# Another order of VectorE's work in Strassen steps, and nine or ten of them in nine projections of a hybrid block

## The chip, the cores and the metric

The kernel runs on one core of one Trainium2 chip. Time is the device time of one execution in microseconds (us); the lower the better. A span is the time from the first to the last instruction of one profiled execution.

## The reference

One decoder block on 256 tokens with 4096 channels, float32. The input is normalized, projected by one large matrix, mixed in two branches, merged under sigmoid gates, projected again and normalized:

```python
h = rmsnorm(x, norm_w)
proj = h @ w_in                              # 4096 -> 6 * 2048 + 2 * 4096
u_p, z_p, u_c, b_c, c_c, z_c, g = split(proj)
y_pool = causal_multiscale_pool(u_p, pool_w, pool_scale) * silu(z_p)
y_conv = b_c * conv3(c_c * u_c) * silu(z_c)
br = [y_pool @ w_branch[0], y_conv @ w_branch[1]]
merged = sum(sigmoid(g + gate_b) * br)
out = rmsnorm(x + merged @ w_out, final_norm_w)
```

Nearly all of the work is in the three large products; the weights come from HBM once.

## The kernel before

**Units and steps.** The products are cut into units of 1024 output columns: cz, cb, cu, cc (twice) for the convolution branch, pz, pu (twice) for the pooling branch, g0_c and g1_c for the gates (c from 0 to 3), then b0_c and b1_c for the branch products and o0 to o3 for the output. A unit of the first product has 16 steps. A step takes 256 of the contracted channels (an "x pair", two blocks of 128 channels by two of 128 tokens) and one weight tile of 128 x 2048, which holds four quarters of 512 columns.

A float32 product is made of three matmuls of rounded operands: high x high, high x low, low x high, where low is the value less its rounded high. A plain step (P) has 8 block products, so 24 matmuls of 512 columns. A Strassen step (S) has 7 products of sums of blocks, so 21 matmuls; it needs four sums of the x blocks (Q3, Q5, Q6, Q7) beside the four blocks, and four sums of the weight quarters. The results of S collect in the `sums` banks (E) and the `shared` banks (F), which are put together at the unit's end ("corner sums", `corner_sums`, and `combine`).

**What prepares a step.** SyncE loads the weight tile into one of three `raw` tiles (L75). ScalarE rounds quarters to high parts in the `ring` tile (`highs`, L57), VectorE subtracts for the low parts (`lows`, L60). The ring has 15 cells, a cell being one quarter's high and low; P takes 4 cells, S takes 3 for quarters (`rounded`) and 4 for sums (`split`). Between these two, `added` makes the four sums of quarters in a tile `parts` (128 x 4 x 512). A cell is free again when TensorE has used it for the last time, so the ring bounds how far ScalarE and VectorE can run ahead. A raw tile is free when its last reader is done.

**Order.** Every engine works in program order. A planner at build time emits the instructions: `multiply` emits a step's matmuls, `pump` emits preparation for up to four steps ahead when ring cells are free, and `tick` (every 6 matmuls) emits one item of a queue of side work, such as a unit's epilogue (`epi`: activations, taps, transposes, stores) or a "fill", which loads a stored y or m block, makes its sums and its high and low parts. When a bank closes, `evacuate` has ScalarE copy it to SBUF; that copy stands in ScalarE's queue behind what was emitted before.

**Texts.** The order of P and S within a unit is a text of 16 letters (L36 to L46): FIRST and SIX4 for cz and pz0, EIGHT for cb, cc, pu, EIGHT3 for cu, HOST for pz1 and g0_0 (with steps of the pooling branch in between), NINE for the other gate units, SEVEN3 for g1_3. `seq_x` turns a text into x pairs: pairs 0 to 7 are laid out for P, pairs 8 to 15 for S. In a NINE unit pair 7 serves as the ninth S; its four sums stand in a tile of their own, `ninth` (128 x 2 x 4 x 128), which is made during g0_0 from a second load of the pair (`gate_unit`), and the class `Operand` finds them in `entry`. Pair 15 stands in a tile `last_pair`; all others in `arena`.

The places in the code that the change and the steps of the prediction touch: the texts (L36 to L46), `entry` (L186), `added` (L274) and `split` (L281), the table of products in `groups` (L305), `evacuate` (L386), `seq_x` (L488), `taps` (L527), `conv_units` (L513), `pool_units` (L550), `gate_unit` (L651), and the opening of tiles between units.

Of the kernel before, what the change touches and what calls it, by code (L numbers as in the profile page):

```python
# [9 lines left out]
F32 = mybir.dt.float32  # L10
# [27 lines left out]
SEVEN3 = "PPPSPSPSPSPSPSPS"  # L38
EIGHT3 = "PPPSSPSPSPSSPSPS"
EIGHT = "PSPSPSPSPSPSPSPS"  # L40
NINE = "PSPSPSPSSPSPSSPS"
HOST = "PPPBPPMMPSPSSPSSPSS"
OUT3 = "PSPSPSPSPSPSSPPP"
# [6 lines left out]
def hybrid_block(ctx: ExitStack, tc: tile.TileContext, x, xc, prm, rows_in, w_in, pool_w, w_branch, w_out, out):  # L50
# [89 lines left out]

    ninth = {}
    last_pair = {}
# [19 lines left out]
    class Operand:  # L162
# [23 lines left out]
        def entry(self, i):  # L186
            if self.kind == "P":
                return (ninth["tile"][:, 0, i], ninth["tile"][:, 1, i]) if i < 4 else (
                    self.view[:, 0, i - 4], self.view[:, 1, i - 4])
            return self.view[:, 0, i], self.view[:, 1, i]  # L190
# [44 lines left out]
    class Step:  # L235
# [25 lines left out]
        def rest(self):  # L261
# [11 lines left out]
            if self.kind == "S":  # L273
                def added(_):  # L274
                    q = self.q
                    add(sums[:, 0:2], q[:, 3:4].to_broadcast([P, 2, NH]), q[:, 1:3])
                    add(sums[:, 2], sums[:, 0], q[:, 2])
                    add(sums[:, 3], sums[:, 2], q[:, 0])
                    lows(self.cells, q[:, 0:3])

                def split(cells):  # L281
                    self.sum_cells = cells
                    highs(cells[0:2], sums[:, 0:2])
                    highs(cells[2:4], sums[:, 2:4])
                    lows(cells, sums)

                return [(None, None, added)] + self.mid + [(4, None, split)]
# [17 lines left out]
        def groups(self):  # L305
# [20 lines left out]
            else:  # L326
# [5 lines left out]
                         "N7": (Q7, w[0], ("F", 1, 0)),  # L332
                         "N6": (Q6, w[2], ("F", 1, 1)),
                         "N4": (A22, w[3], ("E", 1, 1))}
                order = ("M2", "N3", "N4", "M1", "N7", "N5", "N6") if self.closing else (
# [152 lines left out]
    def seq_x(text):  # L488
        if text is FIRST:
            return [("P", i) for i in FIRST]  # L490
        if text is NINE:
            ps, ss = list(range(ND - 1)), list(range(ND, ND + NS + NB)) + [ND - 1]
            return [(c, (ss if c == "S" else ps).pop(0)) for c in text]
        return sequence(text, ND, ND + NS + NB, NB)
# [18 lines left out]
    def conv_units(c, first):  # L513
# [7 lines left out]
        def c_epi(u):  # L521
# [21 lines left out]

        in_unit(f"cz{c}", base + 3 * HALF, lambda u: silu_y(False), FIRST if first else SIX4, dst=Y)
        in_unit(f"cb{c}", base + HALF, b_epi, EIGHT).urgent = lambda: mul(E, E, Y)
        u = in_unit(f"cu{c}", base, lambda u: rescale(Y) + (band_items(0) if c == 0 else []), EIGHT3, dst=Y)
        u.late, u.rotates = True, False
        in_unit(f"cc{c}", base + 2 * HALF, c_epi, EIGHT).urgent = lambda: mul(E, E, Y)

    def pool_units(c):  # L550
        u = in_unit(f"pz{c}", HALF + c * NU, lambda u: silu_y(c == 1) + (gap(4) + band_items(1) if c else []),
                    HOST if c else SIX4, dst=Y)
        if c:
            u.late, u.rotates = True, False
        in_unit(f"pu{c}", c * NU, lambda u: [], EIGHT).urgent = lambda: None

# [94 lines left out]
    def gate_unit(n, c):  # L651
        def epi(u):
            def bias(t):
                gather(E[:, t], gate_b[n, None, c * NU:(c + 1) * NU].to_broadcast([P, NU]))

            def ninth_in():
                move(sa[:, 4:].rearrange("p o c -> p (o c)"), xc[ND - 1])

            def ninth_scaled():
                for k in range(2):  # L660
                    v = sa[:, 6 - 2 * k:8 - 2 * k]
                    act(v, v, scale=norm_col(2 * (ND - 1) + k))

            def ninth_high():
                act(ninth["tile"][:, 0], sa[:, 0:4])

            def ninth_low():
                sub(ninth["tile"][:, 1], sa[:, 0:4], ninth["tile"][:, 0].bitcast(F32))

            pause = gap(12)  # L670
            if (n, c) == (0, 0):
                ninth_in()
                pause = [ninth_scaled, None, lambda: sums_s(sa)] + gap(3) + [ninth_high, None, ninth_low] + gap(3)
# [375 lines left out]
    def run_step(u, st):  # L1049
# [8 lines left out]
        for i, g in enumerate(gs):  # L1058
# [3 lines left out]
            after_group(u, g[0], st)  # L1062

    for u in units:
        if u.name == "b0_0":
# [4 lines left out]
        if u is names["g1_0"]:  # L1070
            bands_open.close()
            ninth["stack"] = ExitStack()
            ctx.enter_context(ninth["stack"])
            pool = ninth["stack"].enter_context(tc.tile_pool(name="ninth", bufs=1))
            ninth["tile"] = pool.tile([P, 2, 4, P], F32R, name="ninth")
        if u is last_x:
            ninth["stack"].close()
            more = ctx.enter_context(tc.tile_pool(name="more", bufs=1))
            stages.append(more.tile([P, 8, P], F32, name="sb"))
            queue_fills()  # L1080
        if u is last:
            break
        for st in u.steps:
# [24 lines left out]
    for st in lead:  # L1108
# [19 lines left out]
    def finish_half(t, n):  # L1128
# [3 lines left out]
            accum_out=ossq[:, t, 3 + n:4 + n])  # L1132
        mul(rest[:, t, cs], E[:, t, cs], Y[:, 0, cs])

    def finish(t):
        r = rout[:, t:t + 1]
        rstd_of(ossq[:, t:t + 1], r, f"rout{t}")
        for c in range(4):
            v = rest[:, t] if c == 3 else parked[c][:, t]
            if c == 1:  # L1140
# [3 lines left out]
        for c in (1, 0, 2, 3):  # L1144
            v = rest[:, t] if c == 3 else parked[c][:, t]
            queue_ = nc.scalar if c == 1 else nc.sync
# [53 lines left out]
```

## Time and profile before

| | |
|---|---|
| Median of three runs | 2384.67 us (2381.68 to 2386.14) |
| The profiled execution's own time | 2381.34 us |
| Its span | 2379.6 us |
| Granted TensorE clock, mean | 0.998 |
| HBM traffic over the span | 229 GB/s |

The profile names engines PE (TensorE's matmuls), PEld (its weight loads), DVE (VectorE), ACT (ScalarE), POOL (GpSimd) and SP (SyncE). A row of the timeline gives start in us, length in us, engine, line, operation, output<-input, shape and how many were merged into it; in brackets stands how long its engine was idle before it, and for whom. A group's row gives busy us and mean ns of one. L57, L60, L72 and L75 are the helpers that issue ScalarE's activations, VectorE's two kinds of elementwise operations and SyncE's loads; L999 is the matmul in `multiply`. Durations of matmuls overlap, so distances between starts are used for their pace. The lines themselves stand in the prediction.

### The profile page before, as it was taken

What the parts mean: (1) busy time and instruction counts of PE and PEld (TensorE: products, weight loads), DVE (VectorE), ACT (ScalarE), POOL (GpSimd) and SP (SyncE); (2) the same over time, 40 slices, a digit from 0 to 9 for tenths busy, and PEclk for the clock granted to TensorE, in tenths of its full rate; (3) what the DMA queues carried; (4) which work ended last, traced back from release to release, by engine and by line L of the source; (5) the groups of instructions that cost most, each with busy time, mean ns of one, the idle gap of its engine ahead of it and who ended that gap; (6) DMA issues with size and microseconds to landing.
All of it is one profiled execution on the core that took longest, in us unless ns stands there. A gap on an engine that the chain in (4) does not pass through costs nothing.

```text
span 2379.6 us, 26984 instructions
## 1 busy us (share of the span) xinstructions
PE 2362.8 (99%) x10493; PEld 1951.2 (82%) x10493; DVE 2147.0 (90%) x1793; ACT 1464.1 (62%) x1427; POOL 109.5 (5%) x168
## 2 busy tenths in 40 slices
PE   9999999999999999999999999999999999999998
PEld 7888888888888888888888888888878888888886
DVE  8789989989979969969999999998998798899998
ACT  6655656656656556656666666666665566566664
POOL 0000100000000000100000000001100000000000
PEclk9999999999999999999999999999999999999999
DMA  9646746656646646746877787678866666767767
GB/s 348 233 181 230 231 164 241 232 201 227 224 177 219 242 176 213 239 175 222 261 241 248 246 259 241 224 264 258 268 270 233 253 232 237 260 207 257 256 217 269
DMA packets 89056, 557.82 MB, mean 234 GB/s; under 512 B 9888, under 2 KB 10144, under 8 KB 28000
## 3 DMA queue, kind: packets, MB, share of 16 engines
q1 hardware_dynamic: 69824, 485.39, 56.3%
q0 software_dynamic: 18528, 69.48, 10.9%
q8 instruction: 82, 1.34, 0.2%
q10 hardware_dynamic: 576, 1.24, 0.1%
q14 instruction: 46, 0.38, 0.0%
HBM read 519.36 MB, written 26.21 MB: 229 GB/s over the span
## 4 chain that ended last, share of the span: by engine, by line
PE 89%; DVE 6%; ACT 2%; DMA 1%; issue 1%; SPq 0%; DVEq 0%; ACTq 0%
PE sums L999 66%; PE shared L999 21%; DVE ring L60 3%; DVE parts L60 1%; DMA raw<-in_w_in_dram 1%; PE shared L636 1%; ACT ring L57 1%; PE shared L444 1%; DVE Y L72 0%; DMA raw<-in_w_branch_dram 0%; ACT E L57 0%; DVE E L72 0%; ACT raw L57 0%; DVE raw L60 0%; DVE E L60 0%
## 5 line engine op out<-in xcount | busy, mean ns | idle before, releaser
L999 PE MATMUL sums<-ring,arena 128*128 128x512 f32 x7377 | 1721.0, 390 | 4.6 <-ACT E L57 3.0
L999 PEld LDWEIGHTS sums<-ring,arena 128*128 128x128 f32 x7377 | 1383.3, 188 | 294.5 <-ACT E L57 3.4
L60 DVE TENSOR_TENSOR ring<-raw,ring 128x1536 fp32r<-128x1536 f32 (+3 forms) x529 | 933.5, 1777 | 131.1 <-ACT ring L57 130.5
L57 ACT ACTIVATE ring<-raw 128x2048 fp32r<-128x2048 f32 (+3 forms) x528 | 786.6, 1506 | 407.8 <-PE sums L999 214.9
L57 ACT ACTIVATE ring<-parts 128x1024 fp32r<-128x1024 f32 (+1 forms) x427 | 421.3, 1002 | 366.3 <-DVE parts L60 328.9
L999 PE MATMUL shared<-ring,arena 128*128 128x512 f32 x2142 | 515.3, 389 | 0.0
L60 DVE TENSOR_TENSOR ring<-parts,ring 128x2048 fp32r<-128x2048 f32 (+3 forms) x243 | 458.5, 1901 | 30.4 <-ACT ring L57 29.9
L999 PEld LDWEIGHTS shared<-ring,arena 128*128 128x128 f32 x2142 | 402.0, 188 | 83.6
L60 DVE TENSOR_TENSOR parts<-parts,raw 128x512 f32<-128x512 f32 x398 | 275.8, 693 | 13.6
L60 DVE TENSOR_TENSOR parts<-raw 128x1024 f32<-128x1024 f32 x199 | 242.7, 1219 | 6.0 <-DMA raw<-in_w_in_dram 5.3
L999 PE MATMUL sums<-ring,last_pair 128*128 128x512 f32 x336 | 83.7, 396 | 0.0
L999 PEld LDWEIGHTS sums<-ring,last_pair 128*128 128x128 f32 x336 | 63.2, 188 | 15.1
L999 PE MATMUL shared<-ring,last_pair 128*128 128x512 f32 x192 | 47.6, 396 | 0.0
L57 ACT ACTIVATE E<-sums 128x512 f32<-128x512 f32 x72 | 41.8, 596 | 7.4 <-PE sums L999 3.5
L999 PEld LDWEIGHTS shared<-ring,last_pair 128*128 128x128 f32 x192 | 36.1, 188 | 8.8
L60 DVE TENSOR_TENSOR raw<-raw 128x512 f32<-128x512 f32 (+1 forms) x33 | 28.7, 869 | 9.1 <-ACT raw L57 8.3
L57 ACT ACTIVATE E<-sums,rin 128x512 f32<-128x512 f32 x28 | 17.8, 688 | 23.7 <-PE sums L999 23.7
L60 DVE TENSOR_TENSOR E<-E,Y 128x2048 f32<-128x2048 f32 x13 | 29.7, 2287 | 0.1
L84 POOL DMA_DIRECT2D E<-Y x14 | 17.0, 1452 | 260.6 <-DVE Y L60 125.0
L60 DVE TENSOR_TENSOR E<-E,last_pair 128x2048 f32<-128x2048 f32 x12 | 27.4, 2286 | 1.4 <-ACT E L57 1.4
L57 ACT ACTIVATE last_pair<-shared 128x512 f32<-128x512 f32 x44 | 24.0, 596 | 7.4 <-PE shared L444 6.5
L57 ACT ACTIVATE Y<-shared 128x512 f32<-128x512 f32 x44 | 23.9, 602 | 5.1 <-PE shared L444 4.6
(133 smaller groups left out, 674.4 us busy)
## 6 DMA issues: line engine op xcount, KB each, us to landing
raw<-in_w_in_dram SPq DMA_DIRECT2D x318, 1024.0 KB, 4.8
raw<-in_w_branch_dram SPq DMA_DIRECT2D x64, 1024.0 KB, 4.9
raw<-in_w_out_dram SPq DMA_DIRECT2D x64, 1024.0 KB, 5.0
E<-in_rows_dram POOLq DMA_DIRECT2D x16, 512.0 KB, 8.9
gates_d<-E POOLq DMA_DIRECT2D x8, 1024.0 KB, 6.8
E<-Y POOLq DMA_DIRECT2D x14, 512.0 KB, 10.0
y_d<-E POOLq DMA_DIRECT2D x8, 512.0 KB, 4.8
raw<-in_pool_w_dram SPq DMA_DIRECT2D x4, 1024.0 KB, 6.7
```

The source lines that it names most:

```text
L57: return pin(nc.scalar.activation(dst, src, func, **kw))
L60: return pin(nc.vector.tensor_tensor(out=dst, in0=a, in1=b, op=op))
L84: return pin(nc.gpsimd.dma_start(dst, src, accum_op=ALU.add))
L444: pin(nc.tensor.transpose(shared(j)[:, i * T + t * P:i * T + (t + 1) * P], src[:, t, c:c + P], ident))
L636: pin(nc.tensor.matmul(o, a, b, start=(k, i) == (0, 0), stop=(k, i) == (3, 2)))
L999: pin(nc.tensor.matmul(ps, lhs, rhs, start=n == 0, stop=n == u.total[b] - 1))
```

## The change

1. In an S step two of the four sums of weight quarters are no longer written to `parts` but over quarters 3 and 2 of the raw tile. VectorE's order becomes: the first two sums, the low of quarter 2, the third sum, the lows of quarters 0 and 1, the fourth sum, and after `split`'s three activations the lows of the sums in two halves. `parts` shrinks to two quarters (4 KB a partition less).
2. In the freed room a second tile `eighth` holds the four sums of x pair 7. It is made during cb0 (items behind cz0's epilogue). `ninth` now holds those of pair 6, made during g0_0 as before.
3. cb, cc and pu get nine S steps instead of eight (NINE_A, NINE_B), g0_1 to g0_3 ten instead of nine (TEN); g1_3 gets six instead of seven (SIX4). EIGHT3 (cu) keeps eight in another order.
4. The taps of cc's epilogue alternate between two blocks. The tail's `rest` tile becomes two tiles, with two loads and two adds.

```diff
-EIGHT3 = "PPPSSPSPSPSSPSPS"
+EIGHT3 = "PPPSPSPSSPSPSSPS"
 EIGHT = "PSPSPSPSPSPSPSPS"
 NINE = "PSPSPSPSSPSPSSPS"
+NINE_A = "PSPSSPSPSSPSPSPS"
+NINE_B = "PSPSPSPSSPSPSSPS"
+TEN = "PSPSSPSSPSSPSSPS"
...
-                return (ninth["tile"][:, 0, i], ninth["tile"][:, 1, i]) if i < 4 else (
-                    self.view[:, 0, i - 4], self.view[:, 1, i - 4])
+                sums_ = side[self.region[1]]
+                return (sums_[:, 0, i], sums_[:, 1, i]) if i < 4 else (self.view[:, 0, i - 4], self.view[:, 1, i - 4])
...
                 def added(_):
                     q = self.q
-                    add(sums[:, 0:2], q[:, 3:4].to_broadcast([P, 2, NH]), q[:, 1:3])
-                    add(sums[:, 2], sums[:, 0], q[:, 2])
-                    add(sums[:, 3], sums[:, 2], q[:, 0])
-                    lows(self.cells, q[:, 0:3])
+                    add(sums, q[:, 3:4].to_broadcast([P, 2, NH]), q[:, 1:3])
+                    lows(self.cells[2:3], q[:, 2:3])
+                    add(q[:, 3], sums[:, 0], q[:, 2])
+                    lows(self.cells[0:2], q[:, 0:2])
+                    add(q[:, 2], q[:, 3], q[:, 0])
 
                 def split(cells):
                     self.sum_cells = cells
-                    highs(cells[0:2], sums[:, 0:2])
-                    highs(cells[2:4], sums[:, 2:4])
-                    lows(cells, sums)
+                    highs(cells[0:2], sums)
+                    highs(cells[3:4], self.q[:, 3:4])
+                    highs(cells[2:3], self.q[:, 2:3])
+                    lows(cells[0:2], sums)
+                    lows(cells[2:4], self.q[:, 2:4])
...
-                         "N6": (Q6, w[2], ("F", 1, 1)),
-                         "N4": (A22, w[3], ("E", 1, 1))}
+                         "N6": (Q6, w[3], ("F", 1, 1)),
+                         "N4": (A22, w[2], ("E", 1, 1))}
...
-        if text is NINE:
-            ps, ss = list(range(ND - 1)), list(range(ND, ND + NS + NB)) + [ND - 1]
+        ns = text.count("S")
+        if ns > NS + NB:
+            ps, ss = list(range(16 - ns)), list(range(ND, 16)) + list(range(ND - 1, 15 - ns, -1))
...
+    def side_items(i):
+        def scaled():
+            for k in range(2):
+                v = sa[:, 6 - 2 * k:8 - 2 * k]
+                act(v, v, scale=norm_col(2 * i + k))
+
+        move(sa[:, 4:].rearrange("p o c -> p (o c)"), xc[i])
+        return [scaled, None, lambda: sums_s(sa)] + gap(3) + [
+            lambda: act(side[i][:, 0], sa[:, 0:4]), None,
+            lambda: sub(side[i][:, 1], sa[:, 0:4], side[i][:, 0].bitcast(F32))]
...
-                for i in range(2):
-                    b = 2 * j + i
-                    kb = 8 * c + b
-                    for s in (1, 2):
+                for s in (1, 2):
+                    for i in range(2):
+                        b = 2 * j + i
+                        kb = 8 * c + b
...
-        in_unit(f"cz{c}", base + 3 * HALF, lambda u: silu_y(False), FIRST if first else SIX4, dst=Y)
-        in_unit(f"cb{c}", base + HALF, b_epi, EIGHT).urgent = lambda: mul(E, E, Y)
+        in_unit(f"cz{c}", base + 3 * HALF, lambda u: silu_y(False) + (gap(4) + side_items(ND - 1) if first else []),
+                FIRST if first else SIX4, dst=Y)
+        in_unit(f"cb{c}", base + HALF, b_epi, NINE_B if c else NINE_A).urgent = lambda: mul(E, E, Y)
...
-        in_unit(f"cc{c}", base + 2 * HALF, c_epi, EIGHT).urgent = lambda: mul(E, E, Y)
+        in_unit(f"cc{c}", base + 2 * HALF, c_epi, NINE_A).urgent = lambda: mul(E, E, Y)
...
-        in_unit(f"pu{c}", c * NU, lambda u: [], EIGHT).urgent = lambda: None
+        in_unit(f"pu{c}", c * NU, lambda u: [], NINE_B).urgent = lambda: None
...
-        text = HOST if (n, c) == (0, 0) else SEVEN3 if (n, c) == (1, 3) else NINE
+        text = HOST if (n, c) == (0, 0) else SIX4 if (n, c) == (1, 3) else TEN if n == 0 else NINE
...
-                sums = ctx.enter_context(tc.tile_pool(name="parts", bufs=1)).tile([P, 4, NH], F32, name="parts")
+                _, sums = open_pool("parts", [P, 2, NH], F32)
+                eighth, side[ND - 1] = open_pool("eighth", [P, 2, 4, P], F32R)
...
-            rest = sums.rearrange("p (t a) n -> p t (a n)", t=2)
-            move(rest, xrows[:, :, 3 * NU:])
+            more.close()
+            eighth.close()
+            rest = [sums, open_pool("rest", [P, 2, NH], F32)[1]]
+            for t in range(2):
+                rest[t] = rest[t].rearrange("p a n -> p (a n)")
+                move(rest[t], xrows[:, t, 3 * NU:])
...
-            queue.extend([None] * 4 + [lambda: add(E, E, rest), lambda: act(root_, rin[:, 0:1], AF.Sqrt)])
+            queue.extend([None] * 4 + [lambda: [add(E[:, t], E[:, t], rest[t]) for t in range(2)], lambda: act(root_, rin[:, 0:1], AF.Sqrt)])
```

More of the change, by code (lines that the diff above doesn't have):

```diff
@@ L38 @@
 SEVEN3 = "PPPSPSPSPSPSPSPS"
-EIGHT3 = "PPPSSPSPSPSSPSPS"
+EIGHT3 = "PPPSPSPSSPSPSSPS"
 EIGHT = "PSPSPSPSPSPSPSPS"
 NINE = "PSPSPSPSSPSPSSPS"
+NINE_A = "PSPSSPSPSSPSPSPS"
+NINE_B = "PSPSPSPSSPSSPSPS"
+TEN = "PSPSSPSSPSSPSSPS"
 HOST = "PPPBPPMMPSPSSPSSPSS"
@@ L139, in hybrid_block @@
     LAST = ("s", NS + NB - 1)
-    ninth = {}
+    side = {}
     last_pair = {}
@@ L654, in bias @@
                 gather(E[:, t], gate_b[n, None, c * NU:(c + 1) * NU].to_broadcast([P, NU]))
[L656 to L673, printed above, removed]
+            pause = side_items(ND - 2) + gap(3) if (n, c) == (0, 0) else gap(12)
             return (rescale(E) if u.late else gap(1)) + [lambda: bias(0), lambda: bias(1)] + pause + [
@@ L1062, in run_step, with open_pool @@
             after_group(u, g[0], st)
+    def open_pool(name, shape, dt):
+        stack = ExitStack()
+        ctx.enter_context(stack)
+        return stack, stack.enter_context(tc.tile_pool(name=name, bufs=1)).tile(shape, dt, name=name)
     for u in units:
@@ L1071, in hybrid_block @@
             bands_open.close()
[L1072 to L1075, printed above, removed]
+            ninth, side[ND - 2] = open_pool("ninth", [P, 2, 4, P], F32R)
         if u is last_x:
-            ninth["stack"].close()
-            more = ctx.enter_context(tc.tile_pool(name="more", bufs=1))
-            stages.append(more.tile([P, 8, P], F32, name="sb"))
+            ninth.close()
+            more, second = open_pool("sb", [P, 8, P], F32)
+            stages.append(second)
             queue_fills()
@@ L1132, in finish_half @@
             accum_out=ossq[:, t, 3 + n:4 + n])
-        mul(rest[:, t, cs], E[:, t, cs], Y[:, 0, cs])
+        mul(rest[t][:, cs], E[:, t, cs], Y[:, 0, cs])
     def finish(t):
@@ L1138, in finish @@
         for c in range(4):
-            v = rest[:, t] if c == 3 else parked[c][:, t]
+            v = rest[t] if c == 3 else parked[c][:, t]
             if c == 1:
@@ L1144, in finish @@
         for c in (1, 0, 2, 3):
-            v = rest[:, t] if c == 3 else parked[c][:, t]
+            v = rest[t] if c == 3 else parked[c][:, t]
             queue_ = nc.scalar if c == 1 else nc.sync
```

## The prediction

> **What bounds the kernel now.** I read the page's head and chain first, then TensorE's waits, then the chain of work in order of time, then the windows of single projections.
>
> ```profile
> span 2379.6 us, 26984 instructions
> ...
> PE 2362.8 (99%) x10493; PEld 1951.2 (82%) x10493; DVE 2147.0 (90%) x1793; ACT 1464.1 (62%) x1427; POOL 109.5 (5%) x168
> ...
> PE 89%; DVE 6%; ACT 2%; DMA 1%; issue 1%; SPq 0%; DVEq 0%; ACTq 0%
> ```
> ```profile
> PE sums L999 <- ACT E L57: 3.0, 1, 3.0
> ...
> PE sums L999 <- ACT Y L57: 0.7, 2, 0.5
> ```
> ```profile
> 105.60 7.48 PE sums L999 x33
> ```
> The reader is to see a kernel that TensorE bounds: 99% busy, 89% of the chain, hardly a wait. Since matmuls overlap, their pace is read from the chain: 33 in 7.48 us, **0.2267 us each**. So a matmul less is worth 0.2267 us, as long as VectorE (90%) keeps its lead.
>
> ```profile
> 95.92:177.67 81.75, 81.75 (x361) 67.58 (x360) 65.85 (x48) 49.39 (x44) 0.00 (x0) 1.00 0.50 180
> 428.50:510.40 81.90, 81.88 (x360) 67.69 (x361) 72.73 (x54) 49.06 (x43) 0.00 (x0) 1.00 0.58 207
> 1204.72:1285.94 81.22, 81.22 (x358) 67.02 (x357) 76.36 (x59) 53.41 (x50) 4.71 (x5) 1.00 0.75 246
> 1611.00:1693.00 82.00, 82.00 (x362) 67.73 (x362) 74.54 (x67) 53.93 (x54) 10.87 (x16) 1.00 0.83 266
> 1693.30:1738.60 45.30, 42.34 (x187) 34.72 (x185) 41.03 (x45) 30.53 (x34) 5.58 (x9) 1.00 0.87 304
> ```
> These windows are cb0, cb1, g0_1, g1_3 and b0_0. Columns: length, then busy time of PE, PEld, DVE, ACT, POOL; GB/s last. VectorE is free for 15.9 us of cb0, 9.2 of cb1, 4.9 of g0_1.
>
> **TensorE's part.** A plain step is 24 matmuls, a Strassen step 21. Nine units get one more Strassen step (cb, cc and pu, two each, and g0_1 to g0_3), g1_3 one less: 8 x 3 = 24 matmuls, 24 x 0.2267 = **-5.44 us**.
>
> ```profile
> L999 PE MATMUL sums<-ring,arena 128*128 128x512 f32 x7377 | 1721.0, 390 | 4.6 <-ACT E L57 3.0 <-DVE ring L740 0.8 <-ACT Y L57 0.7
> ...
> L57 ACT ACTIVATE ring<-raw 128x2048 fp32r<-128x2048 f32 x204 | 390.9, 1917 | 175.3 <-PE sums L999 91.6 <-PE shared L999 25.1 <-DMA raw<-in_w_in_dram 20.4
> ...
> L57 ACT ACTIVATE ring<-raw 128x1536 fp32r<-128x1536 f32 x209 | 311.2, 1489 | 204.3 <-PE sums L999 113.4 <-DMA raw<-in_w_in_dram 44.3 <-issue 23.7
> ...
> L57 ACT ACTIVATE ring<-parts 128x512 fp32r<-128x512 f32 x58 | 33.6, 624 | 30.1 <-DVE parts L60 30.0
> ...
> L999 PE MATMUL shared<-ring,ninth 128*128 128x512 f32 x54 | 13.6, 396 | 0.0
> ```
> Matmuls whose weights lie in the separate tile of sums last 396 ns, not 390. Nine more steps use such a tile, 12 matmuls each: 108 x 6 ns = **+0.7 us** (0 to 1).
>
> **VectorE's part of a Strassen step.** The timeline gives the old order; a start-to-start distance is what an instruction really takes.
>
> ```profile
> 519.35 2.28 DVE L60 TENSOR_TENSOR ring<-raw,ring 128x2048 fp32r<-128x2048 f32 x1
> ...
> 521.55 1.22 DVE L60 TENSOR_TENSOR parts<-raw 128x1024 f32<-128x1024 f32 x1
> ...
> 522.80 1.42 DVE L60 TENSOR_TENSOR parts<-parts,raw 128x512 f32<-128x512 f32 x2
> ...
> 524.14 1.75 DVE L60 TENSOR_TENSOR ring<-raw,ring 128x1536 fp32r<-128x1536 f32 x1
> 524.32 1.07 ACT L57 ACTIVATE ring<-parts 128x1024 fp32r<-128x1024 f32 x1 [0.39 <-PE shared L444]
> ...
> 525.81 2.29 DVE L60 TENSOR_TENSOR ring<-parts,ring 128x2048 fp32r<-128x2048 f32 x1
> ...
> 528.13 1.23 DVE L60 TENSOR_TENSOR parts<-raw 128x1024 f32<-128x1024 f32 x1
> ```
> Old: 1.25 (add of 1024) + 1.34 (two adds) + 1.67 + 2.20 (2048, as at 519.35) = 6.46 us; a plain step is 2.20. Now what instructions cost that don't read their predecessor's result:
>
> ```profile
> 388.04 2.35 DVE L60 TENSOR_TENSOR ring<-raw,ring 128x1024 fp32r<-128x1024 f32 x2
> 390.31 1.91 DVE L72 SCALAR_TENSOR_TENSOR Y<-E,par,Y 128x255 f32<-128x255 f32 x4
> 392.13 1.22 DVE L60 TENSOR_TENSOR parts<-raw 128x1024 f32<-128x1024 f32 x1
> ```
> ```profile
> 532.40 2.29 DVE L60 TENSOR_TENSOR ring<-parts,ring 128x2048 fp32r<-128x2048 f32 x1
> ...
> 534.60 2.35 DVE L60 TENSOR_TENSOR ring<-raw,ring 128x512 fp32r<-128x512 f32 x2
> 534.78 2.43 PE L999 MATMUL shared<-ring,arena 128*128 128x512 f32 x10
> ```
> Two of 1024 end after 2.35, so the first took 2.35 - 1.22 = 1.13, against 1.25 for the add that the next one reads. The pair at 534.60 is 512 and 1536 wide: 2.35 - 1.75 = 0.60, while the first of two dependent adds took 1.42 - 0.69 = 0.73. The new order puts another instruction behind every add: 1.13 + 0.60 + 0.60 + 1.13 + 0.60 + 1.13 + 1.13 = 6.32. **VectorE gains 0.14 us per Strassen step**, although two instructions come in. The taps (1.82 us for four from 390.31) lose two such pairs, some 0.2 us a call. These gains lie beside TensorE and count only where VectorE is late.
>
> The Trainium skill, "VectorE: DVE Perf Modes", section "The DRAIN you can't avoid", speaks against this: the next operation waits until the pipe is empty, and authors are told to keep the number of operations small. The trace doesn't agree, by 1.25 against 1.13. By the page two more operations would cost two more fixed parts and win nothing, an estimate of some 6.6 us a step; this is rival C's mechanism.
>
> Does the lead hold? A ninth step adds 6.32 - 2.20 = 4.12 us; the others give back 8 x 0.14. cb1: 72.73 + 3.0 = 75.7 of 81.3 us. Ten in g0_1: 76.36 + 4.12 - 9 x 0.14 = 79.2 of 80.6. That is tight (1.4 us free), but the unit between two such units keeps nine steps and can win the lead back. So I put no stall there (bounds 0 and 2 us a unit; the upper one is five times the 0.4 us of ScalarE's queue, below). In cu the early pair of Strassen steps leaves little: the lows end at 532.40 + 2.29 = 534.69, and the matmuls from 534.78 on use them. The new text moves that pair back, which can only help.
>
> The second x pair's sums cost cb0 a DMA on POOL, three ScalarE instructions and, on VectorE, these two groups:
>
> ```profile
> 1711.08 1.02 DVE L60 TENSOR_TENSOR sa<-sa 128x128 f32<-128x128 f32 x4
> ```
> ```profile
> L60 DVE TENSOR_TENSOR ninth<-sa,ninth x1: 685/685/685, 1173.1 to 1173.1; 128x512 fp32r<-128x512 f32 x1
> ```
> That is 1.7 us, hidden in cb0's 15.9 free ones even beside its ninth step: nothing (1.7 us at most without that cover). POOL has 0.00 busy in cb0, so its DMA passes nothing; g0_0 prepares the other pair with the same instructions at the old place. The two-part tail (two adds for one of 2048) is 2 x 1.13 - 2.20 = 0.06 us on VectorE, while TensorE still runs: nothing.
>
> **ScalarE's queue.** Old: the last split activation starts at 524.32, 2.77 us after the step's first add, and ends at 3.84. New: the last add starts 1.13 + 0.60 + 0.60 + 1.13 = 3.46 after it, lasts 0.69, and the activation of 512 takes 0.62: 4.8. So what stands behind it on ScalarE comes **1.0 us later** when VectorE is the late one: the next step's highs, and at the start of some units the banks' evacuation, for which TensorE waits. The highs of a plain step (1.92) then end at 6.7 us, 0.4 after VectorE has finished the Strassen step at 6.32: up to 0.4 us of VectorE's time per such pair, where the ring doesn't hold it anyway. And where a load lands late, highs (1.49) and first add (1.13) start together, so the first low, with the whole step behind it on VectorE, waits 0.4 us. TensorE sees either only where the lead is gone.
>
> ```profile
> 1734.23 1.22 DVE L60 TENSOR_TENSOR parts<-raw 128x1024 f32<-128x1024 f32 x1
> ...
> 1737.01 1.06 ACT L57 ACTIVATE ring<-parts 128x1024 fp32r<-128x1024 f32 x1 [0.41 <-DVE parts L60]
> 1737.97 2.04 ACT L57 ACTIVATE E<-sums 128x512 f32<-128x512 f32 x4
> ...
> 1738.61 1.66 PE L999 MATMUL sums<-ring,arena 128*128 128x512 f32 x6 [2.97 <-ACT E L57]
> ```
> ```profile
> 428.52 7.11 PE L999 MATMUL sums<-ring,arena 128*128 128x512 f32 x30 [0.22 <-ACT Y L57]
> ```
> At cb1 (0.22 us now) and pu0 (the 0.5 above) VectorE arrives 1 to 1.5 us earlier through taps and order, ScalarE's group ends 1.0 later: I take +0.4 us together (-0.7 to +2).
>
> b1_0 is the large one: 2.97 us. Its cause starts in g1_3:
>
> ```profile
> 1630.73 0.63 ACT L57 ACTIVATE arena<-sa 128x512 fp32r<-128x512 f32 x1 [6.84 <-DMA sa<-y_d]
> 1631.39 0.69 DVE L60 TENSOR_TENSOR arena<-sa,arena 128x512 fp32r<-128x512 f32 x1 [5.01 <-ACT arena L57]
> ```
> ScalarE waits 6.84 us for a stored y, VectorE 5.01 behind it, and then VectorE is late until b1_0. Behind this place the old text has six Strassen and five plain steps, the new one five and six: VectorE gains 4.12 + 5 x 0.14 = 4.8 us there, TensorE takes 0.7 longer. g1_3 now also ends with a plain step, so its corner banks close a step earlier, and the corner sums stop delaying b0_0. Less some of the 0.4 us waits I carry 4 us to 1734.23, less the 1.0 of the longer queue: 3 us, which is the whole wait. Some is lost where the ring, not VectorE, sets the pace: **-2.5 us** (+1.0 to -3.0).
>
> **Loads.** A raw tile is now read until the step's last low: 2.2 us longer (one instruction of 2048).
>
> ```profile
> ACT ring L57 <- DMA raw<-in_w_in_dram: 77.9, 40, 9.3
> ```
> ```profile
> raw<-in_w_in_dram SPq DMA_DIRECT2D x318, 1024.0 KB, 4.8
> ```
> Three tiles serve steps of 10.2 us a pair: 15.3 us a round. 4.8 of load, 1.5 of highs, 6.3 of VectorE's step: 12.6, so 2.7 us are left for a load that lands late. SP carries only these loads, so nothing else queues behind. I take +0.5 us for single late loads (0 to rival D).
>
> **The sum**, against the profiled execution (2381.34 = span 2379.60 + 1.74 around it): -5.44 + 0.7 + 0.4 - 2.5 + 0.5 = -6.3, so 2375.0. The median of the runs shown, 2384.67, lies 3.33 above that execution: forecast **2378.3 us**, its own range 2374 to 2381.
>
> **Rivals.**
> A (0.50): as summed.
> B (0.25): the wait in b1_0 doesn't go, since the ring or the loads (b0_0 has 304 GB/s, the most of these windows) hold b0_0 back, and the longer queue adds 1.0: -5.44 + 0.7 + 1.0 + 0.4 + 0.5 = -2.8, 2381.8. For it: VectorE already idles 4.3 us in b0_0.
> C (0.10): the order frees nothing, and each instruction pays its fixed part. Split without a gain, 1536 goes from 1.67 to 1.73, 2048 from 2.20 to 2.26: 6.58 a step. Then ten-step units need 76.36 + 4.38 + 9 x 0.12 = 81.8 of 80.6 us: 3 x 1.2 more than B, 2385.4. Against it: the two distances above.
> D (0.15), slower: the raw tile's longer hold. It decides once a load lands over 2.7 us later than the 4.8, as in the busy stretches at unit starts, and the lead there is under 2 us (cu, cz1, pz0, and the nine changed units after their corner sums). Thirteen such places at 1 us: 2381.8 + 13 = 2395.
>
> About 0.2% (4.8 us) is what a measurement of this kernel can tell from no change. Faster by more than that: A without its upper edge and a bit of B, 0.50. Within: the rest of A and B, and C, 0.34. Slower: D and C's edge, 0.16. The range goes from -8.4 (the whole wait and the small ones gone) with 2 us of scatter, 2374, to C with its scatter, 2387.5; it leaves out D.
>
> **What would show it.** Right: 10469 matmuls; 0.60 and 1.13 between VectorE's starts in Strassen steps; no TensorE wait over 1 us near b1_0; units cb, cc and pu 0.6 us shorter, g0_1 at 80.6 us. Wrong: TensorE waits for ScalarE's or VectorE's ring inside g0_1 to g0_3 (C), ScalarE's wait for raw loads well above 77.9 us (D), the wait of 2.97 still there (B).

## The result and the profile after

The changed kernel takes **2395.07 us** (median of four runs, 2393.72 to 2397.51), the kernel before 2384.19 beside it (four runs): ratio 1.0047, 95% interval 1.0030 to 1.0065. It is slower by about 11 us. The forecast was 2378.3; the time came out where rival D, the raw tile's longer hold, had put it.

The page of the changed kernel:

```profile
span 2393.4 us, 27789 instructions
...
PE 2364.1 (99%) x10469; PEld 1948.8 (81%) x10469; DVE 2174.2 (91%) x2221; ACT 1510.7 (63%) x1648; POOL 110.5 (5%) x170
...
PE 88%; DVE 5%; DMA 3%; ACT 2%; issue 2%; POOL 0%; SPq 0%; DVEq 0%; ACTq 0%; POOLq 0%
```

The 24 matmuls are gone, and yet TensorE is busy a little longer. In the chain DMA has gone from 1% to 3%. TensorE's waits (total us, times, longest):

```profile
PE sums L1001 <- DVE ring L63: 5.1, 3, 1.8
PE sums L1001 <- ACT Y L60: 4.8, 2, 2.6
PE sums L1001 <- ACT E L60: 4.5, 2, 3.9
```

Before there were 0.7 for Y and 3.0 for E; 1.8 of VectorE's row is the kernel's opening. The units that the change was made for have become shorter. The windows of cb0, of g0_1, and of a stretch at the start of cb1:

```profile
96.17:177.38 81.21, 81.21 (x359) 67.02 (x357) 70.67 (x72) 53.75 (x58) 0.00 (x0) 1.00 0.50 188
1207.71:1288.34 80.63, 80.63 (x355) 66.46 (x354) 79.54 (x82) 56.47 (x63) 4.71 (x5) 1.00 0.75 248
```
```profile
430.36:434.00 3.64, 3.64 (x9) 2.95 (x10) 3.63 (x4) 3.48 (x4) 0.00 (x0) 0.54 0.02 5
```

cb0 fell from 81.75 to 81.21 us, g0_1 from 81.22 to 80.63. (For cb1 and the two pu units the kernel has the text NINE_B = "PSPSPSPSSPSSPSPS"; the diff above prints that of NINE there.) The third row shows something else: nine matmuls in 3.64 us, about 0.4 us each, at a granted clock of 0.54.

To see where the time is, I took every unit's length from the starts of its matmuls, subtracted the matmuls' own time (0.2267 us each), and compared with before. Four places stand out, three passages between units and the end. The table (us; the other kernels are the experiments below) has the difference that comes from the number of matmuls, those of the four places, the rest, and their sum beside the difference of the spans; what is missing lies ahead of the first matmul or behind the last. "Half" counts matmuls that start about 0.43 us after the one ahead of them.

| kernel | matmuls | cz1, cb1 | pz0, pu0 | g1_3, b0_0, b1_0 | o3 | rest | sum | span | half |
|---|---|---|---|---|---|---|---|---|---|
| before | 0 | 0 | 0 | 0 | 0 | 0 | 0 | 0 | 7 |
| after | -5.4 | +4.1 | +1.9 | +6.8 | +4.5 | +1.9 | +13.8 | +13.8 | 26 |
| order_in_raw | 0 | +5.8 | +2.4 | +5.3 | +2.0 | +0.3 | +15.8 | +17.0 | 27 |
| order_in_parts | 0 | +0.5 | +0.3 | +4.0 | 0.0 | -0.1 | +4.7 | +4.7 | 10 |
| hold_alone | 0 | +7.2 | +5.2 | +3.4 | +1.0 | +0.5 | +17.3 | +18.5 | 27 |
| apart_late | -5.4 | +2.5 | +2.5 | +3.1 | 0.0 | +2.0 | +4.7 | +4.8 | 1 |
| evac_apart_g | -5.4 | +0.5 | +0.5 | +0.2 | 0.0 | +3.6 | -0.7 | -0.9 | 8 |

A row is one profiled execution. The fastest and slowest run of one kernel lie 2 to 6 us apart (11 in the kernel before, with two late ones), so a cell of 1 or 2 us may be chance.

The first place, cz1 to cb1, in the timeline of the changed kernel, and below it the same place before:

```profile
424.45 1.49 ACT L60 ACTIVATE ring<-raw 128x1536 fp32r<-128x1536 f32 x1 [3.80 <-DMA raw<-in_w_in_dram]
424.52 1.23 DVE L63 TENSOR_TENSOR parts<-raw 128x1024 f32<-128x1024 f32 x1 [2.37 <-DMA raw<-in_w_in_dram]
...
429.10 0.63 ACT L60 ACTIVATE ring<-raw 128x512 fp32r<-128x512 f32 x1 [0.24 <-DVE raw L63]
429.64 1.83 ACT L60 ACTIVATE Y<-sums,rin 128x512 f32<-128x512 f32 x3
430.36 0.96 PE L1001 MATMUL sums<-ring,arena 128*128 128x512 f32 x2 [2.57 <-ACT Y L60]
```
```profile
422.96 1.48 ACT L57 ACTIVATE ring<-raw 128x1536 fp32r<-128x1536 f32 x1
...
425.77 2.12 ACT L57 ACTIVATE ring<-parts 128x1024 fp32r<-128x1024 f32 x3
427.80 1.83 ACT L57 ACTIVATE Y<-sums,rin 128x512 f32<-128x512 f32 x3
```

Read the brackets upwards: TensorE waits 2.57 us for the copies of its banks to Y. These stand in ScalarE's queue behind the split of cb1's step 1, the split behind VectorE's sums, and both engines had waited for that step's load, 3.80 and 2.37 us. Before, ScalarE ran through from 422.96 on without waiting and reached the copies just as the banks closed, so there was hardly any slack, and any later landing shows. The loads of raw around this place, after and before (the last row gives their time to landing):

```profile
L78 SPq DMA_DIRECT2D raw<-in_w_in_dram x3: 327/328/328, 407.0 to 417.8; - x3
...
DMA to landing us min/median/max: 6.7/6.9/7.3
```
```profile
L75 SPq DMA_DIRECT2D raw<-in_w_in_dram x3: 327/328/328, 405.2 to 415.7; - x3
...
DMA to landing us min/median/max: 4.8/4.8/4.8
```

They are issued about 2 us later, as the hold says (2.2 in the prediction), but they also need 6.9 us instead of 4.8: together some 4 us late.

The longer landing has a pattern. At this place the kernel before issues its loads one by one, at 405.23, 411.47 and 415.73 us; in the changed kernel tiles come free in pairs, and two loads go out 2.2 us apart, at 407.03 and 409.23, while GpSimd's queue loads `E` from 405.38 to 410.44. I sorted the changed kernel's weight loads after 100 us by what ran beside them for over 1 us. The median landing is 4.8 us for one alone (62 loads), 4.9 beside another weight load only (217), 5.0 beside a transfer of GpSimd's queue only (41), and 6.7 beside both (107). Over the whole stretch the hold does not lengthen loads: 109 take more than 6 us, 110 did before. It changes which ones do.

### The profile page after: what moved, and what is told of

Read it like the earlier page. It is cut to its first block, busy times and chain, and to the rows that moved or that the text cites. A ratio compares the mean times of both kernels' runs of the same rounds, so it can differ in the third digit from the quotient of the medians.

```text
span 2393.4 us, 27789 instructions
## 1 busy us (share of the span) xinstructions
PE 2364.1 (99%) x10469; PEld 1948.8 (81%) x10469; DVE 2174.2 (91%) x2221; ACT 1510.7 (63%) x1648; POOL 110.5 (5%) x170
## 4 chain that ended last, share of the span: by engine, by line
PE 88%; DVE 5%; DMA 3%; ACT 2%; issue 2%; POOL 0%; SPq 0%; DVEq 0%; ACTq 0%; POOLq 0%
PE sums L1001 65%; PE shared L1001 21%; DVE ring L63 2%; ACT ring L60 1%; DMA raw<-in_w_in_dram 1%; DMA raw<-in_w_out_dram 1%; DVE raw L63 1%; PE shared L655 1%; PE shared L450 1%; DMA raw<-in_w_branch_dram 1%; DMA sa<-y_d 1%; DVE parts L63 0%; DVE E L63 0%; ACT E L60 0%; ACT raw L60 0%
## 5 line engine op out<-in xcount | busy, mean ns | idle before, releaser
L1001 PE MATMUL sums<-ring,arena 128*128 128x512 f32 x7230 | 1694.1, 390 | 14.0 <-ACT Y L60 4.8
L1001 PEld LDWEIGHTS sums<-ring,arena 128*128 128x128 f32 x7230 | 1356.9, 188 | 301.1 <-ACT E L60 6.0
L63 DVE TENSOR_TENSOR ring<-raw,ring 128x1024 fp32r<-128x1024 f32 (+3 forms) x948 | 1212.0, 1288 | 149.8 <-ACT ring L60 140.2
L60 ACT ACTIVATE ring<-raw 128x512 fp32r<-128x512 f32 (+3 forms) x951 | 1030.0, 1109 | 487.2 <-DVE raw L63 182.0
L60 ACT ACTIVATE ring<-parts 128x1024 fp32r<-128x1024 f32 (+1 forms) x220 | 220.9, 1010 | 277.2 <-DVE parts L63 258.7
L63 DVE TENSOR_TENSOR parts<-raw 128x1024 f32<-128x1024 f32 x207 | 252.6, 1220 | 12.0 <-DMA raw<-in_w_in_dram 10.1
L63 DVE TENSOR_TENSOR ring<-parts,ring 128x1024 fp32r<-128x1024 f32 (+1 forms) x220 | 253.5, 1157 | 4.3 <-ACT ring L60 4.1
L63 DVE TENSOR_TENSOR raw<-raw 128x512 f32<-128x512 f32 (+1 forms) x240 | 170.6, 711 | 9.4 <-ACT raw L60 8.6
L63 DVE TENSOR_TENSOR raw<-parts,raw 128x512 f32<-128x512 f32 x207 | 142.2, 687 | 0.0
L63 DVE TENSOR_TENSOR arena<-sa,arena 128x512 fp32r<-128x512 f32 (+2 forms) x22 | 19.8, 900 | 8.4 <-ACT arena L60 8.1
```

The costliest lines, as they stand in the source:

```text
L60: return pin(nc.scalar.activation(dst, src, func, **kw))
L63: return pin(nc.vector.tensor_tensor(out=dst, in0=a, in1=b, op=op))
L1001: pin(nc.tensor.matmul(ps, lhs, rhs, start=n == 0, stop=n == u.total[b] - 1))
```

## The experiments

**Theory 1**: the raw tile is held until the lows of the sums, its next load is issued later and lands later still, and at a few places nothing covers that. **Theory 2**: the texts are at fault (more Strassen steps, g1_3's six), the order is harmless. **Theory 3**: the third split activation, 1.0 us later, delays what stands behind it on ScalarE. Each was timed beside the kernel before, in 5 or 11 runs; the median of the kernel before was 2383.32 to 2383.57.

| kernel | median us | ratio to before, 95% interval |
|---|---|---|
| order_in_raw | 2397.59 | 1.0059 (1.0046 to 1.0071) |
| order_in_parts | 2385.93 | 1.0011 (1.0002 to 1.0020) |
| hold_alone | 2399.66 | 1.0071 (1.0057 to 1.0085) |
| seven_kept | 2392.25 | 1.0040 (1.0027 to 1.0052) |
| store_later | 2391.52 | 1.0035 (1.0022 to 1.0048) |
| join_in_e | 2392.76 | 1.0040 (1.0028 to 1.0053) |
| apart_late | 2386.46 | 1.0013 (1.0005 to 1.0022) |
| join_apart | 2386.94 | 1.0015 (1.0006 to 1.0024) |
| evac_apart | 2382.13 | 0.9992 (0.9983 to 1.0001) |
| evac_apart_seven | 2380.95 | 0.9990 (0.9981 to 0.9999) |
| evac_apart_g | 2379.25 | 0.9984 (0.9975 to 0.9992) |
| before_evac | 2381.95 | 0.9995 (0.9986 to 1.0004) |

### The order alone, with and without the hold

**order_in_raw** is the kernel before with the change's `added`, `split` and exchange of N6 and N4, nothing else.

> The kernel before with the new order of VectorE's work and the two sums in the raw tile, but all texts, side tiles and the tail as before: 10493 matmuls. Theory 1 (the raw tile is held until the lows of the sums, so loads are issued 2 to 5 us later and TensorE waits at cz1/cb1, pz0/pu0 and in o3's last steps): slower than before by what these places lost in the changed kernel, 2.3 + 1.1 + 1.8 + 4.5 = 9.7 us at most, 2389 to 2394 us, with TensorE gaps of about 2 us ahead of cb1, pu0 and in o3. Theory 2 (the texts with more Strassen steps and g1_3's six are at fault, the order is harmless): within 2 us of before, 2382 to 2386.

**order_in_parts** has the same order, but the tile of four sums:

```diff
-                    add(q[:, 3], sums[:, 0], q[:, 2])
+                    add(sums[:, 2], sums[:, 0], q[:, 2])
...
-                    add(q[:, 2], q[:, 3], q[:, 0])
+                    add(sums[:, 3], sums[:, 2], q[:, 0])
...
-                    highs(cells[3:4], self.q[:, 3:4])
-                    highs(cells[2:3], self.q[:, 2:3])
+                    highs(cells[2:3], sums[:, 2:3])
+                    highs(cells[3:4], sums[:, 3:4])
...
-                    lows(cells[2:4], self.q[:, 2:4])
+                    lows(cells[2:4], sums[:, 2:4])
```

> As order_in_raw, but the third and fourth sums go to the tile of sums as before, so the raw tile is free when the fourth sum is made; three activations in the split, the same order on VectorE. Theory 1 (hold): no loss at cz1/cb1, pz0/pu0 and o3, 2380 to 2385 us, up to 2 us faster than before by VectorE's 0.14 us per step. Theory 3 (the split's third activation and the later last high delay the evacuations and TensorE, whatever the tile): the same loss as order_in_raw, 2389 to 2394.

**hold_alone** keeps the old order and only reads the raw tile once more:

```diff
                     lows(cells, sums)
+                    pin(nc.vector.tensor_copy(side_note, self.q[:, 0, 0:1]))
```

> The kernel before, old order and all four sums in their own tile, with one added VectorE copy of 128x1 from the raw tile behind the lows of the sums, so that the tile is held as long as in the changed kernel (the copy itself costs VectorE about 0.06 us per step and nothing reads it). If the hold alone costs (theory 1): gaps of 2.5 to 3.6 us ahead of cb1 and pu0 and about 2 us in o3, 2392 to 2398 us, as order_in_raw with 2397.6. If the writing of two sums into the raw tile or the third activation costs: within 2 us of the kernel before, 2382 to 2387.

2397.59 against 2385.93: **the hold costs 11.7 us** with the same instructions in the same order, and it costs them without any of the new texts. Held alone, under the old order, it costs 16.3 (2399.66 against 2383.36); the added copies take VectorE 0.06 us each, and cb0, cu0 and cc0 are as long as before. Both losses are larger than theory 1's ranges (2389 to 2394 and 2392 to 2398), and the two kernels' intervals overlap. TensorE's waits of order_in_raw, then of order_in_parts, then of hold_alone:

```profile
PE sums L1002 <- ACT Y L57: 6.1, 2, 3.2
```
```profile
PE sums L1002 <- ACT E L57: 4.2, 2, 4.0
...
PE sums L1002 <- ACT Y L57: 1.4, 2, 0.7
```
```profile
PE sums L1001 <- ACT Y L57: 8.7, 2, 4.5
```

The Y rows are cb1 and pu0. The loads around cz1's end landed after 6.9, 4.9 and 7.0 us (medians of the view shown above for the changed kernel).

So theory 1 holds and theory 2 is not needed. The order by itself does not win anything: order_in_parts is slower than before by 0.11%, just outside the 2380 to 2385 expected. In the table it loses at one place, b1_0:

```profile
1735.05 1.22 DVE L60 TENSOR_TENSOR parts<-raw 128x1024 f32<-128x1024 f32 x1
...
1739.33 0.63 ACT L57 ACTIVATE ring<-parts 128x512 fp32r<-128x512 f32 x1 [1.13 <-DVE parts L60]
1739.86 2.04 ACT L57 ACTIVATE E<-sums 128x512 f32<-128x512 f32 x4
1740.49 2.07 PE L1002 MATMUL sums<-ring,arena 128*128 128x512 f32 x4 [4.03 <-ACT E L57]
```
```profile
1740.50:1744.70 4.20, 4.20 (x10) 3.33 (x11) 4.17 (x6) 3.29 (x5) 0.00 (x0) 0.50 0.61 249
```

From the first add to the end of the last split activation it is 1739.96 - 1735.05 = 4.91 us, 3.84 before: theory 3's 1.0, as forecast. The wait grew from 2.97 to 4.03 us, and ten matmuls behind it ran at half the clock, in 4.20 us instead of 2.27. How much of this one wait is the queue's is not shown: before_evac (below), with unchanged code at this place, waited 1.97.

### One part of the changed kernel undone or moved

**seven_kept** gives g1_3 its seven Strassen steps back.

```diff
-        text = HOST if (n, c) == (0, 0) else SIX4 if (n, c) == (1, 3) else TEN if n == 0 else NINE
+        text = HOST if (n, c) == (0, 0) else SEVEN3 if (n, c) == (1, 3) else TEN if n == 0 else NINE
```

> The changed kernel with g1_3's seven Strassen steps of before, ending with one (3 matmuls fewer than the changed kernel). Theory 1 (the late loads at g1_3's end come from the hold and from the block that landed late at 1635 us): g1_3 and b0_0 lose as much as before, about 2394. Theory 2 (six steps with a plain one at the end put the evacuation behind b0_0's highs): the 4.3 us gap ahead of b0_0 goes and b1_0's wait of about 3 us may come back, 2388 to 2391.

2392.25 lies between the two ranges, and its interval overlaps with the changed kernel's. The trace shows theory 2's move: the 3.9 us wait ahead of b0_0 goes, and b1_0's comes back as 5.3. This is TensorE's wait for E:

```profile
PE sums L1001 <- ACT E L60: 5.3, 1, 5.3
```

So either text pays at this passage, each at its own place.

**store_later** puts five empty items ahead of the store of y_d.

```diff
-... gap(6) + [lambda: mul(E, E, Y), lambda: put(y_d[1, c], chan(E))]
+... gap(6) + [lambda: mul(E, E, Y)] + gap(5) + [lambda: put(y_d[1, c], chan(E))]
```

> The changed kernel with the store of the convolution's result (y_d) 5 items, about 7 us, later, so that the load of cb1's and pu0's step 1 does not run beside it. If the store lengthens that load (6.8 us against 4.4 in the kernel before): cb1's and pu0's first matmuls come 2 to 3 us earlier and the time falls by 3 to 5 us to 2390 to 2392. If the later issue alone decides: gaps of 2.7 to 3 us stay and the time is 2395.

Inconclusive. The store did not move: GpSimd has nothing else to do, so it issues as soon as E is ready, wherever the instruction stands. Its row:

```profile
415.48 1.48 POOL L84 DMA_DIRECT2D y_d<-E  x2 [9.82 <-DVE E L63]
```

In the changed kernel it is 415.79, with the same 9.82. The interval overlaps with the changed kernel's, so 2391.52 tells nothing, and whether the store lengthens the load stays open. The sorting above speaks against the store alone (5.0 us beside one such transfer only).

**join_in_e** lets cz1 and pz0 keep their corner sums in E, not in a raw tile.

```diff
-                FIRST if first else SIX4, dst=Y)
+                FIRST if first else SIX4, dst=Y).rotates = first
...
-        if c:
-            u.late, u.rotates = True, False
+        u.late, u.rotates = bool(c), False
```

> The changed kernel, but cz1 and pz0 put their corner sums into E instead of into one of the three raw tiles, so that all three raw tiles carry weights at these two ends. Theory 1, sharpened (the hold costs where the corner sums take one of the three tiles): the gaps ahead of cb1 and pu0 shrink from 2.96 and 2.66 us to under 1.2 and the half pace behind them goes, 4 to 6 us faster than the changed kernel, 2389 to 2391. If the order of ScalarE's queue makes these gaps: they stay, 2395.

2392.76, again with an interval that overlaps with the changed kernel's, and the waits stay: TensorE waits for the copies to Y 5.8 us in all (4.8 in the changed kernel).

```profile
PE sums L1000 <- ACT Y L60: 5.8, 2, 3.2
```

My sharpened theory, that the corner sums' place makes the hold expensive, falls. cb1's critical load has the raw tile of cz1's last Strassen step, which is free no earlier.

**apart_late** closes `eighth` ahead of g1_3, where it is read no more, and opens two quarters for the third and fourth sums in its room, so the raw tile is freed early again from there on.

```diff
             ninth.close()
+            eighth.close()
+            rest_, apart["tile"] = open_pool("apart", [P, 2, NH], F32)
...
-                    add(q[:, 3], sums[:, 0], q[:, 2])
+                    self.w = apart.get("tile", q[:, 2:4])
+                    add(self.w[:, 1], sums[:, 0], q[:, 2])
...
-                    add(q[:, 2], q[:, 3], q[:, 0])
+                    add(self.w[:, 0], self.w[:, 1], q[:, 0])
```

> The changed kernel, but from g1_3 on (where x pair 7's sums are no longer read) the third and fourth sums go to a tile of their own in the room of these sums, so the hold is short in the branch and output units. Theory 1: o3's 4.5 us and part of the 6.6 us at the end of g1_3 come back, 2385 to 2389 us. If g1_3's loss comes from its text with a plain step at the end alone: only o3's comes back, about 2390.5.

2386.46, within theory 1's numbers: o3's loss is 0.0 in the table and the passage at g1_3 loses less. o3's rows in the changed kernel were these:

```profile
2357.90 0.33 SPq L78 DMA_DIRECT2D raw<-in_w_out_dram  x1
...
2365.20 1.91 ACT L60 ACTIVATE ring<-raw 128x2048 fp32r<-128x2048 f32 x1 [5.39 <-DMA raw<-in_w_out_dram]
...
2369.49 2.08 PE L1001 MATMUL sums<-ring,last_pair 128*128 128x512 f32 x4 [1.83 <-DVE ring L63]
```

The last load goes out at 2357.90, behind the lows of the last Strassen step, and its first reader starts 7.3 us later. Here no bank copies stand between: TensorE waits for VectorE's lows of the late block. At g1_3 to b1_0, 3.1 of the 6.8 us are left in apart_late, without the hold.

**join_apart** has both edits.

> Both edits, apart_late and join_in_e, together. Theory 1: the gains add, 8 to 15 us faster than the changed kernel, 2380 to 2387, and it may beat the kernel before (2384). If the losses have another cause than the hold: over 2390.

2386.94 lies within theory 1's numbers, but the gains do not add: it is as apart_late alone.

### Moving the bank copies ahead of the late split

**evac_apart** is apart_late with this, so that the splits emitted in the last two steps of cz1 and pz0 come behind the copies:

```diff
-                return [(None, None, added)] + self.mid + [(4, None, split)]
+                return [(None, None, added)] + self.mid + [(4, lambda: not keep["split"], split)]
...
+            keep["split"] = u.name in ("cz1", "pz0") and st in u.steps[-2:]
             run_step(u, st)
+            if st is u.steps[-1]:
+                keep.update(split=False, all=False)
```

> apart_late, and the splits that are emitted in cz1's and pz0's last two steps (that of cb1's and pu0's step 1) come behind the four activations that empty the banks, where they stood ahead of them in ScalarE's queue. Join_in_e showed that the corner sums' place doesn't matter; theory 1, mended: the late load reaches TensorE only through ScalarE's queue, in which the bank copies wait behind a split whose load has landed 4 us later. Then the gaps of 2.98 and 3.27 us ahead of cb1 and pu0 go to under 0.7, and the time falls by 4 to 5 us to 2381 to 2383. If the load itself is missing to TensorE: the gap moves into cb1's and pu0's step 1 and the time stays at 2386.5.

2382.13, 4.3 us faster than apart_late. **evac_apart_g** in addition prepares nothing in g1_3's last step:

```diff
-            if work and work[0][0] <= state["limit"]:
+            if work and work[0][0] <= state["limit"] and not keep["all"]:
...
+            keep["all"] = u.name == "g1_3" and st is u.steps[-1]
```

> evac_apart, and in g1_3's last step nothing is prepared ahead, so that its bank copies come ahead of the highs of b0_0 whose loads land late. If those copies' place makes the 2.35 us gap ahead of b0_0: it goes under 0.7, another 1.5 to 2 us faster than evac_apart, 2379 to 2382. If b0_0's own preparation then comes late: the gap moves into b0_0's first steps, no gain or up to 2 us slower.

2379.25: this version beats both kernels. cz1 to cb1 in its timeline:

```profile
425.79 1.49 ACT L60 ACTIVATE ring<-raw 128x1536 fp32r<-128x1536 f32 x1 [3.71 <-DMA raw<-in_w_in_dram]
...
428.61 2.44 ACT L60 ACTIVATE Y<-sums,rin 128x512 f32<-128x512 f32 x4
429.37 2.79 PE L1004 MATMUL sums<-ring,arena 128*128 128x512 f32 x11
...
430.89 1.10 ACT L60 ACTIVATE ring<-parts 128x1024 fp32r<-128x1024 f32 x1
```

The load lands as late as in the changed kernel, ScalarE still waits 3.71 us for it, but the copies now run ahead of the split and TensorE hardly stops. So at cz1 and pz0 the hold reached TensorE through ScalarE's queue.

**evac_apart_seven** (evac_apart with SEVEN3 in g1_3) and **before_evac** (the kernel before with evac_apart's diff) are the controls.

> evac_apart with g1_3's seven Strassen steps of before (3 matmuls fewer). If six steps are better for the passage from g1_3 to the branch units: slower than evac_apart by the wait ahead of b1_0, 4.4 to 5.7 us with a half pace behind it as in order_in_parts and seven_kept, against g1_3's 4.4: within 2 us of evac_apart. If six steps only cost: 3 to 5 us faster, 2377 to 2380.

> The kernel before with the same later splits at cz1 and pz0 as evac_apart, nothing else. In the kernel before the gaps there are 0.70 us and 0.2 us or so; they can go, at most 1 us faster, 2382.5 to 2384. It says how much of evac_apart's gain is open to the kernel before as well.

2380.95: with seven steps in g1_3 the time is that of evac_apart within the intervals, so without evac_apart_g's edit g1_3's six steps bring nothing. 2381.95: the later split alone brings the kernel before 1.6 us, not told from nothing. It is also the fair comparison: with the same order of the copies at cz1 and pz0, evac_apart (2382.13) is no faster than before_evac, although it has 24 matmuls fewer; up to g1_3 it still holds the raw tile.

## Why the prediction was wrong

By places, in the profiled executions: g1_3 to b1_0 was forecast at -2.5 us and came to +6.8; cz1, cb1, pz0 and pu0 at +0.4 and came to +6.0; o3 lay within the 0.5 for late loads and came to +4.5; the rest was forecast at +0.7 and came to +1.9.

**TensorE's part: right.** 10469 matmuls; cb0 0.54 and g0_1 0.59 us shorter, against 0.68 less the dearer matmuls on separate tiles. Seven of the nine units lie clear of the four places and fall short by 0.09 to 0.14 us each; nine such units make 1.0 us, where I had 0.7.

**VectorE's part: right in its price, worthless in time.** The new step in the changed kernel:

```profile
369.52 1.22 DVE L63 TENSOR_TENSOR parts<-raw 128x1024 f32<-128x1024 f32 x1
370.65 0.69 DVE L63 TENSOR_TENSOR ring<-raw,ring 128x512 fp32r<-128x512 f32 x1
371.26 0.69 DVE L63 TENSOR_TENSOR raw<-parts,raw 128x512 f32<-128x512 f32 x1
371.86 1.22 DVE L63 TENSOR_TENSOR ring<-raw,ring 128x1024 fp32r<-128x1024 f32 x1
372.99 0.69 DVE L63 TENSOR_TENSOR raw<-raw 128x512 f32<-128x512 f32 x1
373.60 1.22 DVE L63 TENSOR_TENSOR ring<-parts,ring 128x1024 fp32r<-128x1024 f32 x1
374.73 1.22 DVE L63 TENSOR_TENSOR ring<-raw,ring 128x1024 fp32r<-128x1024 f32 x1
375.87 1.27 DVE L75 SCALAR_TENSOR_TENSOR Y<-E,par,Y 128x255 f32<-128x255 f32 x3
```

375.87 - 369.52 = 6.35 us, forecast 6.32, old 6.46, in distances of 1.13 and 0.60. g0_1's VectorE is busy 79.54 us, forecast 79.2, and no such unit stalls: rival C is out, and the lead held. But order_in_parts has all of this gain and is not faster.

**ScalarE's queue: right in size.** 1.0 us forecast, 4.91 - 3.84 = 1.07 at b1_0 in order_in_parts. The half pace behind it was not foreseen.

**b1_0's wait, the -2.5: this step failed.** In the changed kernel that wait is almost gone (0.57 us), but TensorE now waits earlier:

```profile
1634.96 0.63 ACT L60 ACTIVATE arena<-sa 128x512 fp32r<-128x512 f32 x1 [9.08 <-DMA sa<-y_d]
...
1640.44 1.89 PE L1001 MATMUL sums<-ring,arena 128*128 128x512 f32 x7 [1.47 <-DVE ring L63]
```
```profile
1699.15 2.00 ACT L60 ACTIVATE ring<-raw 128x1536 fp32r<-128x1536 f32 x2 [1.21 <-DMA raw<-in_w_branch_dram]
...
1701.06 0.67 ACT L60 ACTIVATE E<-sums,rin 128x512 f32<-128x512 f32 x1
...
1701.78 1.65 PE L1001 MATMUL sums<-ring,arena 128*128 128x512 f32 x3 [3.89 <-ACT E L60]
```

I followed VectorE's free time to b1_0 and did not ask what g1_3's plain end puts into ScalarE's queue: b0_0's highs, whose load is late, ahead of E's copies. evac_apart_g, which takes those highs out of the way, brought 2.9 us (2382.13 to 2379.25). In every kernel with six steps ScalarE also waited longer for the stored y, 8.4 to 9.1 us against 6.8 before; why was not settled.

**Loads: this is the term that decided.** "I take +0.5 us for single late loads": it was 11.7 under the old texts (order_in_raw less order_in_parts); under the new ones it was not measured whole, and apart_late got 8.6 of it back. The working failed in three places. It took 4.8 us for a load whenever it is issued, but at cz1's end the held loads went out in pairs beside other transfers and took 6.9. It took the slack as a mean over a round: 6.9 is 2.1 late, inside its 2.7, and TensorE waited all the same. And it looked for places with a short lead of TensorE's operands (cu, cz1, pz0, nine units after their corner sums). cz1 and pz0 were right, but the nine units lost nothing in their middle, and cu's 0.35 us came with the new texts (0.00 in hold_alone); g1_3 and o3 were not named. What decided at cz1 and pz0 was whether the copies of closed banks stand behind the late split. So rival D had the cause, the hold, and by chance the time: four places at some 2 to 7 us, half paces included and at g1_3 only partly by the hold, not thirteen at 1, and at cz1 its condition of 2.7 us was not met. My sign for D was bad too: ScalarE's total wait for w_in loads did not rise at all.

```profile
ACT ring L60 <- DMA raw<-in_w_in_dram: 70.9, 36, 9.4
```

It was 77.9 before: a total over the span does not tell a wait that somebody waits behind from one that is covered.

**The tail: costed at nothing,** and its two adds are indeed nothing; but the hold delayed the last load (above), 4.5 us in the profiled execution, 1 to 2 in order_in_raw and hold_alone.

## What to carry to other kernels

Before a buffer is held longer, look up which load takes its place, when that load lands beside the other transfers of that stretch (not at its median), and what stands behind its first reader in each engine's queue. Slack is not the mean over a round: at cz1's end it was near zero in a kernel whose raw tiles had 2.7 us on average. A copy that frees a bank should stand ahead of preparation that may wait for a load: with that order, and the hold gone from the late units, the changed kernel is 4.3 us faster than the kernel before instead of 11 slower. Not all of that is the change's: before_evac has 1.6 of it, and evac_apart_g's edit at g1_3 (2.9) was not tried in the kernel before, so what the ninth and tenth steps are worth stays open.

## What was not expected of the hardware

After some gaps TensorE runs at half its clock, which adds to the price of the gap: nine matmuls in 3.64 us at a granted clock of 0.54 behind the 2.57 us wait at cb1 (quoted above), 1.6 us more than at full pace, and ten in 4.20 at 0.50 behind 4.03 us, 1.9 more. But not behind each: in apart_late at pu0, and in the kernel before behind b1_0's 2.97 us, the clock stayed full. Over the 14 kept traces, all 12 waits of 2.99 us or more ahead of a matmul of `multiply` had six to 13 matmuls at half pace behind them, of the 27 from 1.8 to 2.97 us only seven.

```profile
765.17 2.12 PE L1003 MATMUL sums<-ring,arena 128*128 128x512 f32 x8 [2.87 <-ACT Y L60]
```
```profile
765.20:769.50 4.30, 4.30 (x19) 3.54 (x20) 4.30 (x5) 3.56 (x5) 0.00 (x0) 1.00 0.00 0
```
```profile
1738.61:1743.00 4.39, 4.39 (x19) 3.66 (x20) 4.32 (x4) 3.31 (x5) 0.00 (x0) 1.00 0.70 264
```

The Trainium skill, "TensorE: Matmul & The Clock Gate", section "HAM oscillation — how this bites in real kernels", warns of idle gaps over about 3.4 us. The 4.03 us agree with it; but 2.57 us did it too, and 2.87 and 2.97 did not, so the length of the gap alone does not decide here. The same page of the Trainium skill, section "What's actually happening", has the activity window run free of the kernel; that would fit, though no run here shows the window.
